# Two matmuls instead of three per k-tile and half in a 32-column projection of a two-layer trunk

## The chip, the core and the metric

The kernel runs on one core of a Trainium2 chip. The time is the device time of one execution in microseconds (us); before the change it is the median of three timed runs. One further execution was recorded by the profiler, and all profile lines of this document come from such recordings.

## The reference, cut to what matters

Two groups of positions, 128 context positions and 512 latent positions, go through two layers. Each layer normalizes, modulates (scale and shift from a condition vector), multiplies by an input weight matrix, runs two mixer branches, gates, and multiplies by an output matrix. In the even layer, one branch is a gated linear attention (GLA) whose gates come from a low-rank projection `rb` of 2 x 16 columns:

```python
qa, ka, va, qb, kb, vb, rb, gp = split_cols(h @ w_in, EVEN_SPLITS)   # rb: 2 * GLA_RANK = 32 columns
...
r = rb.reshape(B, T, 2, GLA_RANK)
logit = jnp.einsum('btdr,drk->btdk', r, wg) + bg
g = (jax.nn.log_sigmoid(logit.astype(jnp.float32)) / GLA_NORMALIZER).reshape(B, T, 2, H_B, DK_B)
```

`h` has 2048 features, `h @ w_in` for `rb` is a product of (640 x 2048) by (2048 x 32). Everything is in float32.

## The kernel before, in words

**Layout.** Activations lie with features on the partitions: 2048 features are 16 k-tiles of 128, and each k-tile holds 642 columns: two columns for the shift vectors of the two groups and 640 positions. The columns are worked on in two halves: half 0 has 322 columns (2 shift columns and 320 positions), half 1 has 320 (`cols`). A projection's output chunk is 128 features x 640 positions and accumulates in two PSUM banks, one per half.

**Precision.** Each float32 operand is split into a `hi` part, rounded to the format in which TensorE (PE) takes one pass, and a `lo` part, the remainder. `acth` and `actl` hold the activations' two parts, `whi` and `wlo` the weights'. A product is taken as hi x hi + lo x hi + hi x lo, so three matmuls per k-tile and half (`mm_k`). Plain float32 matmuls exist too, for small sums and transposes; the profile shows two records for each.

**Weights.** They come from DRAM in units of four k-tiles into `wraw`, a buffer of four slots. ScalarE (ACT) writes `whi` (a copy with rounding), then GpSimd (POOL) writes `wlo` by a subtraction. Both go into a ring of 2560 columns, five blocks of 512; a unit frees its space when its last matmul has been issued (`wpump`, `wget`, `wdone`). The rank projection has only 32 columns; its `hi` and `lo` are each written three times side by side, so that M is 96 and the result stands three times on 96 partitions. `gla_rank` turns this into the factors of the gate matmul in `gla_elem`, whose weights `wgs` are prepared for 96 rows in the same way.

**Order.** One Python program writes each engine's instruction order by hand. It walks through a list `acts` of chunks; while it issues a chunk's matmuls it calls `tick` every two k-tiles, which pumps the weights and advances small tasks (generators in `self.tasks`, such as gates, transposes and attention blocks) and one low-priority task that works out the modulation vectors (`ada_task`). A planner (`Pace`) keeps an estimate of when each engine will be done, by fixed costs, and decides from it which step may be issued next; `until` and `bank` let a task wait for an operand or for a free PSUM bank by this estimate. Modulation sums are made either by VectorE (DVE) in one operation, or by POOL (a product, `prod`) and ACT (the sum of that product), when POOL is free by the estimate (`offload`, `collect`). A change of costs early on therefore changes the order of small work later. PSUM banks are shared out by `pj` (three banks for projections here) and `sm` (three banks for small tasks), two more hold modulation rows.

**Around the change.** The first projections of the even layer are six gate chunks, while modulation weights stream in; then comes the rank projection (`add(d["w_rb"], 96, ...)`, chunk of kind "c", `units`), and then for each of four heads k, q and two value chunks. The rank projection's evacuation `lin` multiplies by the row norm `rstd` on DVE and adds the shift on ACT, into `vt`; then `gla_rank` sets the flag `"r"`, for which the first value chunk's evacuation waits.

Of the kernel before, what the change touches and what calls it, by code (L numbers as in the profile page):

```python
# [13 lines left out]
AF = mybir.ActivationFunctionType  # L14
# [5 lines left out]
KT = D // 128  # L20
# [26 lines left out]
LEAD, FIRST = 1, 6  # L47
# [170 lines left out]
class Core:  # L218
# [14 lines left out]
    ("gmlp_gT", 8),  # L233
    ("gla_m1", 128),
    ("gla_mu", 128),
]


class Trunk:
# [9 lines left out]
    def __init__(self, tc, d, es):  # L249
# [32 lines left out]
        at, c = 0, {}  # L282
# [7 lines left out]
        self.bg_g = c["gla_bgT"].rearrange("p (a b) -> p a b", b=4)  # L290
        self.gn, self.mg, self.m1 = c["gla_gT"], c["gmlp_gT"], c["gla_m1"]
        self.mu = c["gla_mu"].bitcast(U32)
        self.act(self.cT, self.cT, AF.Silu)
        self.ident = self.P([128, 128], "ident")
        make_identity(tc.nc, self.ident)
# [239 lines left out]
    def wstart(self, chunks, acts):  # L535
# [15 lines left out]
                        unit(c, j)  # L551
        last = None
        self.both = {c for kind, x in acts if kind == "h" for c in x[:2]}
        seven = {c for kind, x in acts if kind == "s" for c in x}
        for kind, x in acts:
            if kind == "c" and x >= FIRST:
                for k in (0, 4, 8, 12):
                    unit(x, k)
            elif kind == "k":
                seen = set()  # L560
                for c, k in self.skew(*x[:3]):
                    if (c, k - k % 4) not in seen:
                        seen.add((c, k - k % 4))
                        unit(c, k - k % 4)
            elif kind == "h":
                for r in range(2):
                    for c in x[:2]:
                        for k in (0, 4, 8, 12):
                            unit(c, k, r)
            elif kind == "s":  # L570
                last = self.strassen_jobs(*x, last, unit)
# [75 lines left out]
    def wpump(self, force=False):  # L647
# [18 lines left out]
        if job[0] == "add":  # L666
            o, a, b = job[1]()
# [32 lines left out]
            self.live[key] = (a, a + n * M)  # L700
            self.wpat = a + n * M
        hi, lo = hl
        if m < M:
            raw = raw[:, :, None, :].to_broadcast([128, n, M // m, m])
            hi, lo = (x.rearrange("p a (b c) -> p a b c", c=m) for x in hl)
        nc.scalar.activation(hi, raw, AF.Copy)
        eng = nc.vector if key[0] in self.both and self.nsplit % 2 else nc.gpsimd
        eng.tensor_tensor(lo, raw, hi.bitcast(F32), ALU.subtract)
# [52 lines left out]
    def units(self, c, k0, evac):  # L761

        p = []
        for k in range(k0, KT, 4):
            for half in range(2):
                if k == k0:
                    p.append(self.pj())
                for j in range(k, k + 4):
                    self.mm_k(c, j, [(p[half], half)], k0)
                    if j % 2:  # L770
                        self.tick()
                if k + 4 == KT:
                    evac(*((None, p[1]) if half else (p[0], None)))
                    self.drop(p[half])
            self.wdone((c, k, 0))

    @staticmethod
    def skew(c1, c2, order):
# [1307 lines left out]
    def program(self):  # L2086
# [9 lines left out]
        acts = []  # L2096

        def add(w, M, shift, pre, evac):
            seq.append((w, M, shift, pre, evac))
            acts.append(("c", len(seq) - 1))  # L2100
# [77 lines left out]

            return evac

        add(d["w_rb"], 96, True, None, lazy("vt", rows=96, then=lambda x: self.spawn(self.gla_rank(x))))
        for h in range(4):

            def elem(x, h=h):
# [325 lines left out]
        with tc.manual_schedule():  # L2510
# [13 lines left out]
            for kind, x in acts:  # L2524
                if kind == "c":
                    if x >= FIRST:
                        self.chunk(x)
                elif kind == "s":
                    self.spair(*x)
                elif kind == "k":  # L2530
                    self.kpair(*x)
                elif kind == "h":
                    self.hpair(*x)
                else:
                    x()
# [100 lines left out]
def _consts():  # L2636
# [14 lines left out]
        sel[32 * j, 0] = sel[32 * j + 1, 1] = 1  # L2651
    m1 = np.ones((128, 128), f) + np.eye(128, dtype=f)
    mu = (i[:, None] < i[None, :]).astype(f)
    return {"cos": c4, "sin": s4, "emask": em, "sel": sel, "gla_m1": m1, "gla_mu": mu}


def _na_grid():
# [118 lines left out]
```

## Time and profile before

| | |
|---|---|
| median of three timed runs | 2119.41 us (2116.44 to 2121.92) |
| profiled execution, its own time | 2118.93 us |
| its span in the trace | 2117.1 us |
| busy share PE, DVE, POOL, ACT | 97%, 62%, 61%, 51% |
| rank projection in the trace | 144.36 to 158.48 us |

Times in the trace are counted from the span's start. In a group's row stand the source line, the engine, the operation, the tile written and the tiles read, the shapes, the count, the busy time in us and the mean in ns, then the idle time ahead and what ended it. `PEld` are weight loads, which run beside the matmuls of `PE`; `128*96` is a weight block of 128 rows and 96 columns. Matmul durations overlap, so distances of starts tell what one costs. Where helpers issue everything, all rows have the helper's line (L393 is `mm`, L213 the recording layer), and the tiles' names tell the work apart.

### The profile page before, as it was taken

The numbers are of one execution on the slowest core, as the hardware profiler recorded it, in microseconds if no ns is written. First come the engines' busy times: TensorE is split into PE (matmuls) and PEld (weight loads), VectorE is DVE, ScalarE is ACT, GpSimd is POOL, SyncE is SP. The second block draws the span as 40 slices with busy tenths as digits, with TensorE's granted clock in tenths as the row PEclk, the third lists the DMA queues.
The fourth block names the chain that finished last, engine by engine and source line by source line (L and its number), as shares of the span: only waits on it lengthen the run. The fifth ranks groups of instructions, "written<-read, shape, count | busy, mean of one in ns | idle before, by whom it ended". The sixth has DMA issues, their size and how long they took to land. (4 is left out here: it accounts for less than half of the span.)

```text
span 2117.1 us, 40263 instructions
## 1 busy us (share of the span) xinstructions
PE 2058.0 (97%) x14345; PEld 2003.7 (95%) x14345; DVE 1320.0 (62%) x3063; ACT 1071.2 (51%) x2471; POOL 1285.1 (61%) x1082
## 2 busy tenths in 40 slices
PE   7999999999999999999999999999999999999996
PEld 6899999999999999999999999999999999999995
DVE  4856686666556554988666878777454444465335
ACT  5645565454666665543564444444444544454433
POOL 4756564445545544888565656655555577668873
PEclk9999999999999999999999999999999999999998
DMA  9966343336464544576643455444322344354437
GB/s 363 398 226 189 121 158 107 111 119 197 130 206 150 150 136 145 187 229 219 213 130 105 136 160 159 143 139 149 94 81 90 108 139 130 124 202 132 128 95 248
DMA packets 193401, 341.23 MB, mean 161 GB/s; under 512 B 20944, under 2 KB 70192, under 8 KB 193200
## 3 DMA queue, kind: packets, MB, share of 16 engines
q1 hardware_dynamic: 191728, 337.10, 49.4%
q8 instruction: 112, 1.84, 0.4%
q10 hardware_dynamic: 1472, 1.56, 0.2%
q14 instruction: 89, 0.73, 0.1%
HBM read 304.08 MB, written 31.88 MB: 159 GB/s over the span
## 5 line engine op out<-in xcount | busy, mean ns | idle before, releaser
L393 PE MATMUL bank<-acth,whi 128*128 128x320 f32 (+2 forms) x3320 | 1021.5, 318 | 10.6 <-ACT bc L213 2.8
L393 PE MATMUL bank<-actl,whi 128*128 128x320 f32 (+2 forms) x3320 | 994.7, 310 | 3.7 <-DMA actl<-bl_dram 2.1
L393 PE MATMUL bank<-acth,wlo 128*128 128x320 f32 (+2 forms) x3320 | 994.5, 311 | 3.5 <-POOL wlo L213 3.5
L213 POOL TENSOR_TENSOR wlo<-wraw,whi 128x512 fp32r<-128x512 f32 (+1 forms) x452 | 573.6, 1281 | 412.1 <-ACT whi L213 329.8
L393 PEld LDWEIGHTS bank<-acth,whi 128*128 128x128 f32 (+1 forms) x3320 | 617.6, 189 | 20.9 <-ACT bc L213 3.9
L393 PEld LDWEIGHTS bank<-actl,whi 128*128 128x128 f32 (+1 forms) x3320 | 617.4, 189 | 6.9 <-DMA actl<-bl_dram 3.3
L393 PEld LDWEIGHTS bank<-acth,wlo 128*128 128x128 f32 (+1 forms) x3320 | 617.5, 189 | 5.1 <-POOL wlo L213 5.1
L213 POOL TENSOR_TENSOR wlo<-rs,whi 128x384 fp32r<-128x384 f32 x370 | 408.1, 1123 | 183.2 <-ACT whi L213 143.6
L213 ACT ACTIVATE whi<-wraw 128x512 fp32r<-128x512 f32 (+1 forms) x460 | 262.9, 588 | 93.2 <-PE bank L393 60.7
L393 PE MATMUL bank<-eh,wlo 128*128 128x322 f32 (+1 forms) x666 | 207.2, 311 | 2.7 <-POOL wlo L213 2.7
L393 PE MATMUL bank<-eh,whi 128*128 128x322 f32 (+1 forms) x666 | 209.3, 314 | 0.0
L393 PE MATMUL bank<-el,whi 128*128 128x322 f32 (+1 forms) x666 | 206.9, 311 | 0.0
L213 ACT ACTIVATE whi<-rs 128x384 fp32r<-128x384 f32 x370 | 182.0, 514 | 48.5 <-PE bank L393 41.7
L213 DVE TENSOR_TENSOR wraw<-rs 128x768 f32<-128x768 f32 x74 | 98.8, 1335 | 124.7 <-POOL wlo L213 69.9
L213 DVE CUSTOM_DVE_ANT_0 adas<-adas,bank,partg 128x256 bf16<-128x256 f32 (+1 forms) x290 | 156.2, 539 | 12.6 <-DMA adas<-ada_g 5.3
L213 POOL TENSOR_TENSOR prod<-adas,mixrow 128x512 f32<-128x512 f32 x85 | 111.5, 1321 | 70.4 <-ACT prod L213 48.5
L213 ACT ACTIVATE arena<-arena,bc 128x512 f32<-128x512 f32 (+4 forms) x211 | 106.4, 527 | 79.8 <-DVE arena L213 77.0
L393 PEld LDWEIGHTS bank<-eh,wlo 128*128 128x128 f32 x666 | 125.5, 189 | 3.9 <-POOL wlo L213 3.7
L393 PEld LDWEIGHTS bank<-eh,whi 128*128 128x128 f32 x666 | 125.7, 189 | 0.1
L393 PEld LDWEIGHTS bank<-el,whi 128*128 128x128 f32 x666 | 125.8, 189 | 0.0
L213 DVE CUSTOM_DVE_ANT_0 adas<-adas,bank,part 128x512 bf16<-128x512 f32 x151 | 112.4, 744 | 9.8 <-DMA adas<-ada 6.8
L213 ACT ACTIVATE arena<-Y 128x320 f32<-128x320 f32 (+1 forms) x76 | 38.9, 512 | 152.1 <-DVE Y L213 125.9
(218 smaller groups left out, 2480.1 us busy)
## 6 DMA issues: line engine op xcount, KB each, us to landing
wraw<-w_even SPq DMA_DIRECT2D x176, 256.0 KB, 3.4
adas<-ada_g SPq DMA_DIRECT2D x128, 256.0 KB, 3.7
adas<-ada SPq DMA_DIRECT2D x128, 256.0 KB, 3.8
rs<-w_odd SPq DMA_DIRECT2D x50, 384.0 KB, 3.3
wraw<-w_odd SPq DMA_DIRECT2D x74, 256.0 KB, 3.5
wraw<-w_out SPq DMA_DIRECT2D x64, 256.0 KB, 3.9
rs<-w_odd SPq DMA_DIRECT2D x50, 256.0 KB, 3.8
Y<-ada SPq DMA_DIRECT2D x24, 512.0 KB, 7.3
```

The costliest lines, as they stand in the source:

```text
L213: return f(*args, **kw)
L393: self.nc.tensor.matmul(out, lhsT, rhs, start=start, stop=stop, **kw)
```

## The change

The rank projection's unit in the ring is now one block of 64 columns per k-tile, `hi` in the first 32 and `lo` in the other 32, both within `whi`. For each k-tile and half it is multiplied by `acth` and by `actl`, two matmuls with M = 64; this also takes lo x lo, which the three products leave out. A new method `quad` issues it: half 0 over all 16 k-tiles, then half 1, with all four units of weights held until the end; ACT copies each half's bank into a buffer of the ring `gt`. A spawned task then multiplies each copy, in float32, by the constant `rep` (a 32 x 32 identity matrix tiled 4 x 3; its first 64 rows are used), which adds the `hi` and `lo` rows and repeats the sum three times on 96 partitions; the old evacuation works on that result. `rep` comes with the other small constants in one transfer, which grows from 420 to 516 columns.

```diff
--- before.py
+++ after.py
@@ -233,6 +233,7 @@
     ("gmlp_gT", 8),
     ("gla_m1", 128),
     ("gla_mu", 128),
+    ("rep", 96),
 ]
 
 
@@ -290,6 +291,7 @@
         self.bg_g = c["gla_bgT"].rearrange("p (a b) -> p a b", b=4)
         self.gn, self.mg, self.m1 = c["gla_gT"], c["gmlp_gT"], c["gla_m1"]
         self.mu = c["gla_mu"].bitcast(U32)
+        self.rep = c["rep"]
         self.act(self.cT, self.cT, AF.Silu)
         self.ident = self.P([128, 128], "ident")
         make_identity(tc.nc, self.ident)
@@ -551,9 +553,10 @@
                         unit(c, j)
         last = None
         self.both = {c for kind, x in acts if kind == "h" for c in x[:2]}
+        self.stacked = {x for kind, x in acts if kind == "q"}
         seven = {c for kind, x in acts if kind == "s" for c in x}
         for kind, x in acts:
-            if kind == "c" and x >= FIRST:
+            if kind == "q" or kind == "c" and x >= FIRST:
                 for k in (0, 4, 8, 12):
                     unit(x, k)
             elif kind == "k":
@@ -700,9 +703,9 @@
             self.live[key] = (a, a + n * M)
             self.wpat = a + n * M
         hi, lo = hl
-        if m < M:
-            raw = raw[:, :, None, :].to_broadcast([128, n, M // m, m])
-            hi, lo = (x.rearrange("p a (b c) -> p a b c", c=m) for x in hl)
+        if key[0] in self.stacked:
+            hl = hi
+            hi, lo = hl[:, :, :m], hl[:, :, m:]
         nc.scalar.activation(hi, raw, AF.Copy)
         eng = nc.vector if key[0] in self.both and self.nsplit % 2 else nc.gpsimd
         eng.tensor_tensor(lo, raw, hi.bitcast(F32), ALU.subtract)
@@ -773,6 +776,40 @@
                     evac(*((None, p[1]) if half else (p[0], None)))
                     self.drop(p[half])
             self.wdone((c, k, 0))
+
+    def quad(self, c, parts):
+
+        _, M, shift, _, evac = self.chunks[c]
+        units = [(c, k, 0) for k in range(0, KT, 4)]
+        banks = [self.pj(), self.pj()]
+        for half, p in enumerate(banks):
+            cs = self.cols(half, shift)
+            n = cs.stop - cs.start
+            for u in units:
+                w = self.wget(u)
+                for j in range(4):
+                    for i, x in enumerate((self.ah, self.al)):
+                        k = u[1] + j
+                        self.mm(p[:M, :n], w[:, j, :], x[:, k, cs], start=k == i == 0, stop=k == KT - 1 and i == 1)
+                    if j % 2:
+                        self.tick()
+            self.nc.scalar.activation(parts[half][:M, :n], p[:M, :n], AF.Copy)
+            self.drop(p)
+        for u in units:
+            self.wdone(u)
+
+        def work():
+            for half, x in enumerate(parts):
+                cs = self.cols(half, shift)
+                x = x[:M, : cs.stop - cs.start]
+                yield from self.until(x)
+                yield from self.bank()
+                p = self.sm()
+                self.mm(p[:96, : x.shape[1]], self.rep[:M, :], x)
+                evac(*((None, p) if half else (p, None)))
+                yield
+
+        self.spawn(work(), first=True)
 
     @staticmethod
     def skew(c1, c2, order):
@@ -2178,7 +2215,8 @@
 
             return evac
 
-        add(d["w_rb"], 96, True, None, lazy("vt", rows=96, then=lambda x: self.spawn(self.gla_rank(x))))
+        add(d["w_rb"], 64, True, None, lazy("vt", rows=96, then=lambda x: self.spawn(self.gla_rank(x))))
+        acts.append(("q", acts.pop()[1]))
         for h in range(4):
 
             def elem(x, h=h):
@@ -2527,6 +2565,8 @@
                         self.chunk(x)
                 elif kind == "s":
                     self.spair(*x)
+                elif kind == "q":
+                    self.quad(x, [L["gt"].next() for _ in range(2)])
                 elif kind == "k":
                     self.kpair(*x)
                 elif kind == "h":
@@ -2651,7 +2691,8 @@
         sel[32 * j, 0] = sel[32 * j + 1, 1] = 1
     m1 = np.ones((128, 128), f) + np.eye(128, dtype=f)
     mu = (i[:, None] < i[None, :]).astype(f)
-    return {"cos": c4, "sin": s4, "emask": em, "sel": sel, "gla_m1": m1, "gla_mu": mu}
+    rep = np.tile(np.eye(32, dtype=f), (4, 3))
+    return {"rep": rep, "cos": c4, "sin": s4, "emask": em, "sel": sel, "gla_m1": m1, "gla_mu": mu}
 
 
 def _na_grid():
```

## The prediction

> **What bounds the kernel now.** I read the page's list of engines and its slices first, then stretches of the trace, then the groups of the edited instructions, then the waits.
>
> ```profile
> span 2117.1 us, 40263 instructions
> ...
> PE 2058.0 (97%) x14345; PEld 2003.7 (95%) x14345; DVE 1320.0 (62%) x3063; ACT 1071.2 (51%) x2471; POOL 1285.1 (61%) x1082
> ...
> PEclk9999999999999999999999999999999999999998
> ```
>
> TensorE is busy for 97% of the span at full granted clock; the next engine has 62%. Where the missing 3% lie is seen from stretches (columns: length, then busy time and records of PE, PEld, DVE, ACT and POOL, granted clock, DMA share, GB/s):
>
> ```profile
> 0.00:130.00 130.00, 114.35 (x1299) 101.22 (x1300) 80.83 (x160) 71.58 (x161) 77.06 (x69) 0.99 0.96 360
> 130.00:200.00 70.00, 68.34 (x463) 67.77 (x462) 41.20 (x107) 34.23 (x80) 44.01 (x38) 1.00 0.66 203
> 144.36:158.48 14.12, 14.12 (x98) 14.12 (x97) 5.54 (x15) 6.50 (x15) 9.16 (x9) 1.00 0.76 239
> 200.00:420.00 220.00, 215.53 (x1478) 210.45 (x1477) 155.00 (x271) 122.25 (x255) 118.00 (x82) 1.00 0.39 124
> 420.00:800.00 380.00, 375.76 (x2521) 363.40 (x2520) 221.88 (x594) 232.39 (x582) 190.69 (x146) 1.00 0.49 153
> 800.00:1165.00 365.00, 353.90 (x2358) 348.11 (x2358) 265.15 (x580) 180.10 (x391) 249.73 (x214) 1.00 0.56 178
> 1165.00:2065.00 900.00, 897.53 (x6045) 882.89 (x6044) 527.56 (x1307) 414.55 (x977) 589.72 (x522) 1.00 0.41 130
> ```
>
> Up to 130 us the DMA engines are the limit (share 0.96) and PE is idle for 15.6 us. From 130 to 1165 us it is idle for 1.66 + 4.47 + 4.24 + 11.10 = 21.5 us, from 1165 to 2065 us for 2.5 us. The edited projection lies in the third row, 144.36 to 158.48 us, with no PE idle time at all: in that place a matmul less is time less, unless something that PE needs later is not ready sooner.
>
> **What is removed: 32 matmuls.** The projection's first and last matmul, and the first of the next chunk:
>
> ```profile
> 144.36 0.31 PE L393 MATMUL bank<-acth,whi 128*96 128x322 f32 x1
> ...
> 158.33 0.31 PE L393 MATMUL bank<-acth,wlo 128*96 128x320 f32 x1
> 158.48 0.31 PE L393 MATMUL bank<-acth,whi 128*128 128x322 f32 x1
> ```
>
> Between them stand 16 k-tiles x 2 halves x 3 products = 96 matmuls in 14.12 us, 147 ns each. (Durations of 0.31 us overlap; the distance of starts is the price.) The changed kernel issues 16 x 2 x 2 = 64, with 64 weight columns where there were 96 and the same 322 or 320 moving columns. Does the narrower weight block alter the 147 ns? The 463 records of the stretch 130 to 200 us, nearly all 128 columns wide, took 68.34 us, 148 ns each; so 32 columns less moved the distance by 1 ns at most. The loads themselves:
>
> ```profile
> L393 PEld LDWEIGHTS bank<-acth,whi 128*128 128x128 f32 x3288 | 612.5, 189 | 20.9 <-ACT bc L213 3.9 <-DVE arena L213 3.1 <-issue 3.0
> L393 PEld LDWEIGHTS bank<-acth,whi 128*96 128x96 f32 x32 | 5.2, 162 | 0.0
> L398 PEld LDWEIGHTS bank<-ident,arena 128*64 128x64 f32 x16 | 1.8, 111 | 0.0
> ```
>
> They fell from 189 to 162 ns without a shorter distance, so they lie beside the streaming. I take 147 ns: 64 x 0.147 = 9.41 us, a gain of 4.71 us. The ends for the 64-wide distance: 148 ns, and 147 x 111/162 = 101 ns if loads did set it (6.5 us, a gain of 7.6 us). I take the upper end because 96 against 128 columns is the nearest row. [...]
>
> **What is added on PE: two float32 matmuls** that add the hi and lo rows and copy them three times (64 rows in, 96 out, 322 and 320 columns; at most 64 rows of `rep` are read). No such shape is in the trace; the nearest are the float32 sums over ones, two records to a matmul:
>
> ```profile
> 253.57 1.24 PE L393 MATMUL bank<-arena,ones 128*128 128x320 f32 x4
> 254.41 0.55 PE L393 MATMUL bank<-acth,whi 128*128 128x322 f32 x1
> 254.80 0.31 PE L393 MATMUL bank<-actl,whi 128*128 128x322 f32 x1
> ```
>
> The second ordinary matmul starts at 254.80, so the first took its turn at about 254.65, and two float32 matmuls held PE for 254.65 - 253.57 = 1.08 us. By their records alone they end at 254.41 (0.84 us), by their whole duration 1.24 us: the ends. Net on PE: -4.71 + 1.08 = **-3.6 us** (-3.9 to -3.4 with these ends; -6.5 with the other end of the distance).
>
> **The added wait.** Each half's bank is copied to SBUF by ACT before its float32 matmul. Nearest copy, and the queue that could hold it up:
>
> ```profile
> L213 ACT ACTIVATE sums<-bank 128x322 f32<-128x322 f32 x50 | 21.6, 433 | 17.6 <-PE bank L393 17.6
> ...
> L213 ACT ACTIVATE prod<-prod 128x512 f32<-128x512 f32 x104 | 64.6, 622 | 24.9 <-POOL prod L213 24.5
> ```
>
> In the built order, the first float32 matmul stands 6 matmuls of the next chunk behind the projection, the second another 6 behind it. The second half's copy therefore has 12 x 0.147 + 0.54 = 2.3 us to be made; it takes 0.43 us, but two sums of modulation products stand ahead of it on ACT, and those wait for POOL. Everything on PE stands behind these float32 matmuls.
>
> ```profile
> ACT prod L213 <- POOL prod L213: 24.5, 17, 5.1
> ```
> ```profile
> L393 PE MATMUL bank<-r,wgs x16: 302/308/313, 190.4 to 435.6; 96*128 96x320 f32 x16
> ```
>
> I cost the wait at nothing: ACT is busy for 6.50 of 14.12 us there. If that cover is gone, the price is the longest wait for a product less the cover, 5.1 + 0.43 - 2.3 = 3.2 us, which would leave a gain of 0.3 us. The results themselves are not needed early: the gate matmuls first read them at 190 us.
>
> **Weights, banks and DMA.** The four splits shrink from 384 to 128 columns on ACT and POOL. In the changed order all four stand ahead of the shift columns that the projection's first matmul also needs, so their being shorter gains nothing on the path.
>
> ```profile
> L213 POOL TENSOR_TENSOR wlo<-wraw,whi 128x512 fp32r<-128x512 f32 (+1 forms) x452 | 573.6, 1281 | 412.1 <-ACT whi L213 329.8
> ```
>
> All four blocks are now held to the end of the projection (1024 of 2560 ring columns, which leaves three blocks of the next chunk instead of about four); a block lasts PE 24 x 0.147 = 3.5 us and a split takes POOL 1.28 us, so three are cover enough. The `rep` columns make the first small transfer 128 x 96 x 4 B = 49 KB larger: at the 360 GB/s of the first stretch 0.14 us, at most on the path, at least zero; I take 0.1 us.
>
> **What moves.** The host-side planner writes the order, and from here it comes out differently. Comparing the built orders: 30 matmuls fewer of some 13,400 on PE, and the last 6,172 are the same in both, which is the tail from about 1165 us. Before that, only small tasks (transposes, state and gate matmuls) change place by a few matmuls. The modulation products split anew: POOL does 113 instead of 104, VectorE correspondingly fewer.
>
> ```profile
> L213 DVE CUSTOM_DVE_ANT_0 adas<-adas,bank,part 128x512 bf16<-128x512 f32 x151 | 112.4, 744 | 9.8 <-DMA adas<-ada 6.8
> L213 POOL TENSOR_TENSOR prod<-adas,mixrow 128x512 f32<-128x512 f32 x85 | 111.5, 1321 | 70.4 <-ACT prod L213 48.5 <-DMA adas<-gateT 5.8 <-ACT mixrow L213 5.6
> ```
>
> That is 9 x 1.32 = 11.9 us more on POOL, 9 x 0.62 us on ACT and as many short accumulator reads, 9 x 0.74 us less on VectorE. Both have slack over the stretch, so I cost it at nothing; it is the second rival below that uses it.
>
> **Sum.** -4.7 + 1.1 + 0.1 = -3.5 us. The profiled execution took 2118.93 us (span 2117.1 and 1.8 around it), 0.5 us under the median of 2119.41; on the median's level that makes **2115.9 us**, 0.17% less. Timed runs reached from 2116.44 to 2121.92, so about 0.3%, 6.4 us, is what a measurement can tell from no change.
>
> **Rivals.**
> 1. *The new order also loses stalls* (faster). The 21.5 us of PE idle time before 1165 us are drawn anew. The first of them is near the edit:
>
> ```profile
> 176.14 0.41 PE L393 MATMUL bank<-acth,whi 128*128 128x320 f32 x1 [1.56 <-ACT bc L213]
> ```
> ```profile
> 175.40 0.60 ACT L213 ACTIVATE bank<-adas 128x512 f32<-128x512 f32 x1 [2.20 <-DMA adas<-shift_s]
> ```
>
>    There ACT stood at a copy of modulation rows whose DMA was late, and a projection bank came free late. Losing this and one or two more, 5 us in all, gives 2111 us; 2.9 us are enough to pass the bound. Against it: new stalls are as likely as lost ones. 0.20.
> 2. *POOL becomes late* (slower).
>
> ```profile
> PE bank L393 <- POOL wlo L213: 6.2, 8, 1.4
> ```
>
>    Its place is the split of weights from 160 to 1165 us: a product that the planner put in POOL's queue ahead of a `wlo` delays it by 1.32 us, and once the ring's reserve is used up PE waits. All nine: +11.9 us, 2115.9 + 11.9 = 2127.8 us. It decides (over 2125.8) from 9.9 us, eight of nine. For it: PE already waits 8 times for `wlo`, up to 1.4 us. Against: 6.2 us in all. A row makes it dearer:
>
> ```profile
> L213 DVE TENSOR_TENSOR wgs<-arena,wgs x4: 414/886/1359, 147.9 to 375.3; 32x256 fp32r<-32x256 f32 x4
> ```
>
>    The same subtraction takes 414 to 1359 ns, so a VectorE operation can lose 0.9 us, and more POOL work makes this more frequent. [...] 0.13.
> 3. *The gain is absorbed*: PE comes 3.5 us earlier to evacuations, DMAs or copies that don't, the added wait above among them, and stands there. 2119.4 us. Against: PE's idle time in the GLA stage is only 1.66 + 4.47 us in 290. 0.10.
> 4. *Loads set the distance*: a gain of 7.6 - 1.1 - 0.1 = 6.4 us, 2113.0 us, at the bound. [...]
>
> **Numbers.** My forecast has 0.54, with 2112 to 2121 us as its own range (about 4 us of redrawn stalls each way). Faster by over 0.3%: rivals 1 and 4, 0.23; slower: rival 2, 0.13; within: 0.64. To hold 8 in 10 the range reaches into both: 2108.0 (rival 1 with 8 us of stalls gone) to 2126.5 us (rival 2 past its point).
>
> **What would show it.** In the changed profile: 64 matmuls of 128*64 at 147 ns, 9.4 us from first to last; two float32 matmuls of 64*96, together near 1.1 us, with no idle time ahead of them; PE busy time from 130 us on lower by about 3.6 us, and PE idle time from 130 to 1165 us near 21.5 us; the tail from 1165 us unchanged in length. I am wrong if that idle time differs by more than 3 us, if PE waits on `wlo` for much over 6.2 us, or if the 64-wide distance is far from 147 ns.

## The result, and the profile after

The changed kernel took 2126.76 us (median of 5 runs, 2123.49 to 2129.38) against 2120.38 us of before on the same chip (5 runs, 2116.44 to 2121.92): a ratio of 1.0033, with a 95% interval of 1.0018 to 1.0048. It is slower, by 6.4 us. The forecast was 2115.9 us with a range up to 2126.5 us; the measured time is 10.9 us above the forecast and 0.3 us above the end of the range.

The profiled execution took 2129.38 us. The lines of its page that answer those of before:

```profile
span 2127.6 us, 40229 instructions
...
PE 2058.9 (97%) x14317; PEld 2003.3 (94%) x14317; DVE 1321.0 (62%) x3048; ACT 1077.1 (51%) x2488; POOL 1293.9 (61%) x1091
...
PEclk9999999999999999999999999999999999999998
```

On this page nothing seems to have happened: PE is busy for 0.9 us more with 28 records less. (In rows, `arena`, `small`, `bank`, `prod` and `Y` are buffers, `wlo` the weights' low part, `ident` an identity matrix; the bracket gives the idle time ahead of an instruction and what ended it.) The same stretches as before show more (length, then busy time and records of PE, PEld, DVE, ACT, POOL, granted clock, DMA share, GB/s):

```profile
0.00:130.00 130.00, 110.27 (x1275) 96.11 (x1276) 81.91 (x156) 67.94 (x153) 74.15 (x67) 0.99 0.95 352
130.00:200.00 70.00, 67.40 (x430) 64.56 (x429) 35.22 (x93) 36.41 (x87) 42.78 (x39) 0.95 0.65 202
200.00:420.00 220.00, 213.95 (x1466) 210.81 (x1465) 155.95 (x256) 117.65 (x237) 107.35 (x75) 0.98 0.39 117
420.00:800.00 380.00, 375.01 (x2518) 363.72 (x2518) 228.18 (x602) 239.73 (x603) 212.06 (x160) 1.00 0.52 161
800.00:1165.00 365.00, 351.00 (x2310) 343.93 (x2309) 250.25 (x561) 177.69 (x388) 240.17 (x208) 0.98 0.54 174
1165.00:2065.00 900.00, 897.65 (x6048) 882.92 (x6047) 536.34 (x1324) 417.27 (x984) 594.07 (x523) 1.00 0.42 130
148.83:158.20 9.37, 9.37 (x67) 8.64 (x64) 0.90 (x2) 2.15 (x5) 2.51 (x5) 1.00 0.58 193
```

From 130 to 1165 us PE is idle for 2.60 + 6.05 + 4.99 + 14.00 = 27.6 us (21.5 before). The granted clock, 1.00 in all those stretches of before, is 0.95, 0.98, 1.00 and 0.98. After 1165 us the two profiles agree (897.65 and 897.53 us busy of 900). So the loss lies between the projection and 1165 us, in idle time and in the clock. Five short stretches hold the clock's part:

```profile
161.00:169.60 8.60, 6.73 (x23) 5.76 (x23) 4.79 (x12) 5.96 (x16) 6.87 (x6) 0.60 0.59 167
381.00:392.00 11.00, 6.00 (x30) 5.71 (x29) 9.60 (x13) 4.91 (x13) 4.96 (x4) 0.69 0.32 96
815.00:822.00 7.00, 4.27 (x13) 2.56 (x12) 4.26 (x11) 3.57 (x8) 3.85 (x4) 0.76 0.38 116
851.00:860.00 9.00, 6.72 (x35) 6.49 (x34) 5.53 (x10) 4.24 (x11) 5.03 (x4) 0.81 0.26 71
1086.00:1099.00 13.00, 10.21 (x47) 9.27 (x46) 11.76 (x20) 8.74 (x17) 10.23 (x8) 0.74 0.19 59
```

In each, the granted clock fell to half during a stall of PE or within 1.6 us of its end. A stall is here time in which PE has nothing to run because it waits for another engine. The first stall is the wait that the change added; its rows on PE, ACT's queue ahead of it, and the matmuls:

```profile
159.18 0.78 PE L395 MATMUL bank<-arena,small 64*96 64x322 f32 x2
...
160.59 0.63 ACT L213 ACTIVATE prod<-prod 128x512 f32<-128x512 f32 x1 [1.39 <-POOL prod L213]
161.83 0.63 ACT L213 ACTIVATE prod<-prod 128x512 f32<-128x512 f32 x1 [0.51 <-POOL prod L213]
...
162.46 0.41 ACT L213 ACTIVATE arena<-bank 64x320 f32<-64x320 f32 x1
...
162.92 1.38 PE L395 MATMUL bank<-arena,small 64*96 64x320 f32 x2 [1.87 <-ACT arena L213]
```

The second half's copy (162.46) stood behind two product sums that waited for POOL (1.39 and 0.51 us), as the prediction had described, but the cover of 2.3 us was not enough. The other four stalls of PE:

```profile
386.79 0.47 PE L400 MATMUL bank<-ident,Y 128*128 128x128 f32 x1 [5.00 <-DVE Y L213]
...
818.56 1.22 PE L395 MATMUL bank<-arena 128*128 128x512 f32 x1 [2.73 <-ACT arena L213]
...
854.12 0.41 PE L395 MATMUL bank<-acth,whi 128*128 128x320 f32 x1 [2.28 <-DVE arena L213]
...
1089.56 0.56 PE L395 MATMUL bank<-actl,whi 128*128 128x322 f32 x2 [2.22 <-POOL actl L213]
```

Before had no stall above 1.6 us between 130 and 2065 us, and one stretch of half clock there (at 1081.8 us, 3.4 us long, behind stalls of 1.24 and 1.15 us within 3 us).

Matching the projection matmuls of the two traces one by one, from the first of the edited projection on, gives the position of the changed kernel against before (us; negative is ahead; where small tasks have changed place the position swings by several us for a while, so the places given are ones where it has settled, to about 1 us):

```
end of the projection     -4.8
behind the 2nd float32    +2.0    (the added wait, two float32 matmuls, half clock)
at 178 us of before       +0.2
260 to 380 us             -3.0
387 us                    +2.8    (the 5.00 us stall and half clock)
804 us                    +1.2
816 us                    +6.0    (the 2.73 us stall and half clock)
850 us                    +8.1    (the 2.28 us stall and half clock)
1137 us                   +8.9    (the 2.22 us stall and half clock)
```

At 380 us the changed kernel was still ahead by 3.0 us, about what had been forecast, but by another way: it had been 2.0 us behind and regained 5 us, 1.8 us of it at the stall that before has at 176 us. The loss came behind 380 us, at four stalls.

The projection began 4.5 us later than in the profile of before (148.83 against 144.36 us), and behind 1137 us the changed kernel was 2.9 us shorter: 4.5 + 8.9 - 2.9 = 10.5 us, the difference of the spans. The first and the last term are not the change's doing alone: c_const below, with the instructions of before, has a start 4.3 us later and an end 1.7 us shorter too.

### The profile page after: what moved, and what is told of

Same layout as the page of the kernel before. It is cut to its first block, busy times and chain, and to the rows that moved or that the text cites. A ratio compares the mean times of both kernels' runs of the same rounds, so it can differ in the third digit from the quotient of the medians.

```text
span 2127.6 us, 40229 instructions
## 1 busy us (share of the span) xinstructions
PE 2058.9 (97%) x14317; PEld 2003.3 (94%) x14317; DVE 1321.0 (62%) x3048; ACT 1077.1 (51%) x2488; POOL 1293.9 (61%) x1091
## 3 DMA queue, kind: packets, MB, share of 16 engines
q8 instruction: 112, 1.84, 0.4%
## 5 line engine op out<-in xcount | busy, mean ns | idle before, releaser
L395 PE MATMUL bank<-acth,wlo 128*128 128x320 f32 (+1 forms) x3288 | 986.4, 311 | 3.3 <-POOL wlo L213 3.3
L395 PEld LDWEIGHTS bank<-acth,wlo 128*128 128x128 f32 x3288 | 614.4, 190 | 4.6 <-POOL wlo L213 4.6
L213 POOL TENSOR_TENSOR prod<-adas,mixrow 128x512 f32<-128x512 f32 x93 | 122.5, 1326 | 77.2 <-ACT prod L213 43.6
L213 DVE CUSTOM_DVE_ANT_0 adas<-adas,bank,part 128x512 bf16<-128x512 f32 x143 | 106.4, 744 | 18.9 <-DMA adas<-ada 12.9
L213 DVE TENSOR_TENSOR bank<-bank,sums 128x320 f32<-128x320 f32 (+1 forms) x148 | 70.9, 493 | 70.5 <-PE bank L395 55.2
```

The costliest lines, as they stand in the source:

```text
L213: return f(*args, **kw)
L395: self.nc.tensor.matmul(out, lhsT, rhs, start=start, stop=stop, **kw)
```

## The experiments

To compare profiles, I split each at the first matmul of the projection and at the first matmul of the second layer's chunk that reads `eh` (1137.1 us in before): head, middle, rest.

```
            head    middle   rest     time, us (median)   ratio to before
before     144.4    992.7   980.0     2120.4
after      148.8   1001.6   977.1     2126.8              1.0033 [1.0018, 1.0048]
e1_kept    147.2    991.6   978.8     2121.9              1.0015 [1.0006, 1.0024]
e3_late    145.8   1000.2   978.1     2123.3              1.0022 [1.0013, 1.0032]
p1_minus   145.0    993.8   978.0     2121.9              1.0012 [1.0003, 1.0021]
p3_small   145.0   1000.0   980.3     2129.3              1.0055 [1.0036, 1.0073]
e4_wide    144.6    993.9   978.5     2120.5              0.9995 [0.9987, 1.0004]
c_const    148.7    996.6   978.4     2121.0              1.0003 [0.9992, 1.0013]
e5_vector  146.0    992.4   977.5     2120.1              1.0004 [0.9995, 1.0013]
g_before   146.0    981.6   980.6     2108.4              0.9950 [0.9938, 0.9963]
g_edit     147.2    982.1   980.8     2109.3              0.9953 [0.9940, 0.9967]
```

Head, middle and rest come from one profiled execution each, the time from all timed runs, and the ratio is against before on the same chip in the same session (before's median was 2119.1 to 2120.7 us in these sessions). Up to 1137 us s_long and s_spread (below) run the instructions of before, and so does c_const; with before itself their middles are 992.7, 993.9, 992.9 and 996.6 us. So a difference of less than 4 us between two middles says nothing by itself.

My theory after the result, A: the edit gains its 3.6 us, and the planner's new order loses more, in stalls and in the half clock behind them. Against it B: the edit itself costs (the added wait, the float32 matmuls); and C: the larger transfer of constants delays the first 130 us.

### Order alone: the planner charged differently

In p1_minus and p3_small the kernel is before; only the cost that the planner charges for the projection's matmuls is altered, so that it writes another order.

```diff
 def mm(...):
     cost = n / 2190.0 - 0.0008 if ...
+    if r and out.shape[0] == 96:
+        cost *= 0.745          # p1_minus; 0.93 in p3_small
```

> The kernel of before with its old projection; only the planner is told that the projection's matmuls take 25% less (3.6 us), so that the later order is redrawn as by the change. Theory A: the time moves although no work changed, by 2 to 8 us, with the PE stalls and the half-clock stretches of the new order; which sign is not foreseen. Rival B (the edit itself is the cause): 2120.4 us within 1.5 us.

> As the kernel before, the planner is told that the projection takes 7% less (1.0 us). Theory A: the order is redrawn as much as by a large error, so the time moves by 2 to 8 us, in either direction. Rival B: 2120.4 us within 1.5 us.

p3_small took 2129.3 us, 0.55% more than before, with the same 14345 PE records as before; the new order also moved four modulation sums from VectorE to POOL and ACT (108 product sums on ACT where before has 104). That is more than the 2 to 8 us that theory A had allowed. p1_minus came out 0.12% slower (0.03 to 0.21%): the 2121.9 us lie at the edge of what B allowed and under what A asked, so this run decides nothing, although it was told the 3.6 us of the change. A new order can cost much or almost nothing. In p3_small the middle is 1000.0 us, and two of the stalls of the changed kernel stand in the same places:

```profile
384.34 0.47 PE L400 MATMUL bank<-ident,Y 128*128 128x128 f32 x1 [5.02 <-DVE Y L213]
...
815.67 4.54 PE L395 MATMUL bank<-arena 128*128 128x512 f32 x8 [2.72 <-ACT arena L213]
```

Stretches of that profile around them, and the same places in before behind:

```profile
379.00:391.00 12.00, 6.98 (x35) 6.71 (x34) 9.15 (x15) 6.32 (x15) 3.13 (x2) 0.72 0.35 112
813.00:821.00 8.00, 5.33 (x14) 3.39 (x15) 4.26 (x11) 3.02 (x8) 3.82 (x4) 0.79 0.49 164
```
```profile
377.00:389.00 12.00, 10.97 (x80) 10.46 (x79) 8.80 (x14) 7.80 (x17) 5.31 (x4) 1.00 0.50 153
806.00:816.00 10.00, 10.00 (x59) 8.88 (x58) 5.11 (x14) 5.54 (x13) 5.02 (x4) 1.00 0.57 185
```

So an order that differs only because one cost on the host differs by 7% takes at least about as long as the changed kernel. A loss of this size does not need the edit.

### The edit in the old order

e1_kept has the edited projection, but the planner is charged for the old one, so that everything else keeps before's order. The float32 matmuls are put out 6 and 18 matmuls behind the projection. The two halves alternate unit by unit, as in before, so that both banks are finished near the end; in the change half 0 was finished half a projection earlier.

```diff
+ for a, b in ((hi, h), (hi, l), (lo, h)):
+     self.pe(n / 2190.0 - 0.0008, p[half][:M, :n], a, b)      # charge the old three
+ for i, b in enumerate((h, l)):
+     e.tensor.matmul(p[half][:64, :n], hi[:, 0:64], b, ...)   # issue the new two
...
+ self.hooks.append([self.DELAY[half], f])                     # DELAY = (6, 18)
```

> The changed projection (64-wide blocks, two matmuls per k-tile and half, copies, two float32 matmuls), but the planner is charged for the old one: the order of all other work stays that of before. Theory A (the edit itself gains its 3.6 us; the loss comes from the new order, whose longer PE stalls also bring stretches of half clock): 2116.9 us, granted clock as before (0.994), PE idle time from 130 to 1165 us near 21.5 us. Rival B (the edit itself costs: its added wait, the float32 matmuls): 2124 to 2127 us with a half-clock stretch behind the projection. Rival C (the larger constant transfer slows the first 130 us by some 4 us): the projection starts near 148.8 us instead of 144.4, about 2121 us.

It took 2121.9 us, not 2116.9, and is 0.15% slower than before (0.06 to 0.24%). The gain was there at the end of the projection (-4.75 us against before) and gone behind the float32 matmuls (0.0 us). The profile:

```profile
159.98 0.42 ACT L833 ACTIVATE arena<-bank 64x322 f32<-64x322 f32 x1
160.45 0.78 PE L803 MATMUL bank<-arena,small 64*96 64x322 f32 x2 [2.88 <-ACT arena L833]
```

The first half's copy came 2.9 us too late, again behind product sums. Part of A fell with this: the old order alone does not bring the gain to the end. The number alone is nearest to C (2121 us), which c_const tests. This profile is of the fastest of the 11 executions, with a mean granted clock of 0.995; the other ten had 0.993 or 0.994 and took 2120.4 to 2124.6 us, so that there may be half clock behind the stall in those. No profile shows it.

### The float32 matmuls later, in the new order

```diff
+ self.hooks.append([24, f])     # the float32 matmul and its evacuation, 24 matmuls later; planner not told
```

> The changed kernel with its own order, only the two float32 matmuls and the evacuation behind them are issued 24 matmuls (3.5 us) later. Theory A: the PE stall of 1.9 us ahead of the second float32 matmul goes, and with it the half-clock stretch of 6.8 us behind it (3.4 us of work): 2126.8 - 5.3 = 2121.5 us. Rival (the stretch has nothing to do with that stall): 2126.8 - 1.9 = 2124.9 us and the stretch stays.

2123.3 us, a ratio of 1.0022 where the changed kernel has 1.0033: some 2.3 us less and not the 5.3 of theory A, with intervals that overlap. The profile says more than the time: the stall at 161 us and its half clock are gone, the later ones are not (5.01, 2.72 and 2.19 us; the middle is 1000.2 us). Here the price of the float32 matmuls is seen without a stall:

```profile
159.43 0.31 PE L399 MATMUL bank<-acth,wlo 128*128 128x322 f32 x1
159.67 0.78 PE L832 MATMUL bank<-arena,small 64*96 64x322 f32 x2
160.38 0.41 PE L399 MATMUL bank<-acth,whi 128*128 128x322 f32 x1
160.63 0.31 PE L399 MATMUL bank<-actl,whi 128*128 128x322 f32 x1
```

The ordinary matmul of 159.43 has its turn until 0.147 us later, 159.58, and the one of 160.38 until 160.63, so one float32 matmul takes 160.63 - 0.147 - 159.58 = 0.90 us, two 1.8 us. Position against before: -4.76 at the end of the projection, -2.97 behind both. With the wait gone the edit is worth 3.0 us, and the order still loses 10 us from there.

### Larger constants alone

```diff
+    ("rep", 96),      # in the constants of before; read by nothing
```

> Before with the 96 columns of the replication table added to its constants and read by nothing; every engine's instructions are those of before. Theory C (the larger transfer of constants delays the first stage, as the starts of the projection say: 148.8, 147.2 and 145.8 us in the three kernels that carry the table, 144.4 to 145.0 us in the three that don't): projection start 2 to 4 us later than 144.4 us and a time of 2121 to 2123 us. Theory A (the first stage varies from run to run): 2119 us within 1 us, start of the projection 144 to 146 us.

2121.0 us, a ratio of 1.0003 [0.9992, 1.0013]: C, as some 4 us, falls; the interval has room for 2.8 us at most. The profiled execution of this kernel had its projection start at 148.66 us all the same, and a stall of 3.66 us at 178.9 us, with before's instructions; but it was the second slowest of 12 (2125.5 us), and executions of before in the same session spread from 2115.6 to 2125.1 us. The five profiles of kernels that carry the table in their constants start the projection at 145.8 to 148.8 us, the nine others at 144.4 to 147.2 us. By the median of c_const, then, most of the 4.5 us by which the profile after starts later is scatter, its execution being the slowest of the five; that the larger transfer has no part in it is not shown.

### The float32 matmuls later, in the old order; then the copies on VectorE

```diff
- DELAY = (6, 18)                 # e1_kept
+ DELAY = (30, 45)                 # e4_wide; (12, 24) in e5_vector
+ tc.nc.gpsimd.tensor_copy(...)    # rep from the identity, twice; not from the constants
- e.scalar.activation(parts[half][:64, :n], p[half][:64, :n], AF.Copy)
+ e.vector.tensor_copy(parts[half][:64, :n], p[half][:64, :n])      # e5_vector only
```

> The edited projection in the order of before, as in e1_kept, with two alterations: the two float32 matmuls stand 30 and 45 matmuls behind the projection where e1_kept had 6 and 18, and the 32x96 replication table is built on the chip by two small GpSimd copies of the identity and not carried by the constants. Nothing is left out. Theory A (the edit gains 3.6 us of TensorE time and e1_kept lost it again in one stall of 2.88 us, where the copy of the first half's bank stood on ScalarE behind product sums that wait for GpSimd): that stall is gone, and the time is that of e1_kept less 2.9 us, 2119.0 us, or 2117 if e1_kept's later start of the projection (147.15 against 144.36 us) was the larger constant transfer. Theory B (the edit itself costs): 2121 to 2123 us with no stall near the float32 matmuls.

2120.5 us: the same as before, between the 2119.0 us of A and the 2121 to 2123 us of B. The stall moved from the float32 matmul to the next chunk, which needed the bank that the same late copy had not yet given back:

```profile
157.60 0.42 ACT L835 ACTIVATE arena<-bank 64x322 f32<-64x322 f32 x1
158.06 0.41 PE L401 MATMUL bank<-acth,whi 128*128 128x320 f32 x1 [2.13 <-ACT arena L835]
```

> As e4_wide, with the copies of the two banks made by VectorE, where e4_wide has them on ScalarE behind product sums that wait for GpSimd, and the float32 matmuls 12 and 24 matmuls behind the projection. Nothing is left out. In e4_wide TensorE still stood 2.13 us, at the next matmul that needed the bank which the copy had not yet given back. Theory A (the added copy, by its place in ScalarE's queue, is what eats the edit's gain, first through the float32 matmul, then through the bank): no stall above 0.6 us between 150 and 166 us, and 2120.5 - 2.1 = 2118.4 us, some 2 us below before. Theory B (the edit has no gain to give, wherever the copy runs): 2120.5 us, as before.

2120.1 us, again the same as before, as B said. A's condition, no stall over 0.6 us, was not met: VectorE's copy was late by less (1.14 us, behind modulation products that waited for their transfers), and what was left of the gain met the next wait (first row: PE at the float32 matmul; then ACT and PE at the shift row):

```profile
158.47 0.78 PE L805 MATMUL bank<-arena,rep 64*96 64x322 f32 x2 [1.14 <-DVE arena L835]
...
176.00 0.60 ACT L216 ACTIVATE bank<-adas 128x512 f32<-128x512 f32 x1 [2.38 <-DMA adas<-shift_s]
...
176.74 0.41 PE L401 MATMUL bank<-acth,whi 128*128 128x320 f32 x1 [2.20 <-ACT bc L216]
```

It is the stall that the prediction quoted at 176.14 us of before (1.56 us), now 2.20 us: counted from the projection's start PE came 1.7 us earlier and left 1.1 us earlier, so 0.6 us of the gain went there. Positions against before in e5_vector: -4.75 at the end of the projection, -1.7 behind the float32 matmuls, -1.1 at 176 us, -0.9 at 206 us, -0.8 at 256 us, -0.4 at 1137 us.

### Are the transfers what takes the gain back?

Both kernels of this pair bring a quarter of the modulation rows' columns from the fifth transfer of the stage on, and the instructions read old values in the others. g_edit is e5_vector otherwise, g_before is before.

```diff
+ cut = i >= 4 and jobs[0][0] == "b0" and x.shape[1] == 1
+ self.dma(x, y, (x[:, :, :128], y[:, :, :128]) if cut else None)
```

> Before, in which the transfers of modulation rows (the shift rows and the tiles that are multiplied with them) after the first four of the stage from 145 us on bring 128 of their 512 columns; the other 384 columns are left out, and the instructions that read them read old values. Every instruction and its place are those of before. Base for g_edit. Both theories: the stall of TensorE at 174.6 us, which ended on a shift row's transfer, is shorter than its 1.56 us, and the middle (first matmul of the projection to first matmul of the second layer's chunk on the row pieces, 144.36 to 1137.1 us = 992.7 us in before) is 0 to 2 us shorter.

> e5_vector with the same transfers cut to a quarter (the other columns left out), to be compared with g_before. In e5_vector the edit gained only 0.3 us in the middle (992.4 against 992.7 us), and the matmul behind the second stall started at 176.74 us after a shift row that landed late (176.14 us in before). Theory D (the edit's gain is taken back by modulation rows whose transfers set their own pace, at 157 and at 175 us): without that pace TensorE has no stall over 0.6 us at 157 and at 175 us, and the middle is 2.5 to 3.6 us shorter than that of g_before, and so is the time. Theory E (it is lost elsewhere, along the whole stage): still within 1 us of g_before.

D falls. The transfers matter, for both kernels are 10 to 11 us faster. (For g_before 0 to 2 us had been expected; PE's waits for ACT's `arena` fell from 4.8 to 0.8 us and for `wlo` from 4.9 to 1.4 us between 130 and 1165 us.) In g_edit the stalls at 158 and 175 us are down to 0.49 and 0.55 us, and yet its middle is 982.1 us against 981.6 us without the edit. By the five runs each, the means differ by 1.2 us with an interval of -2.1 to +4.4 us; the 2.5 us or more that D forecast as a gain lie outside, though not by much. PE's idle time in the middle is 15.7 us in g_edit and 12.3 us in g_before, 3.4 us more. Some of it:

```profile
158.98 0.78 PE L805 MATMUL bank<-arena,rep 64*96 64x322 f32 x2 [0.49 <-DVE arena L835]
...
175.58 0.41 PE L401 MATMUL bank<-acth,whi 128*128 128x320 f32 x1 [0.55 <-ACT bc L216]
...
837.07 0.41 PE L401 MATMUL bank<-acth,whi 128*128 128x320 f32 x1 [1.18 <-DVE arena L216]
...
959.78 0.41 PE L401 MATMUL bank<-acth,wlo 128*128 128x320 f32 x1 [0.80 <-POOL wlo L216]
```

Its positions against g_before: -4.75, -2.4 behind the float32 matmuls, -1.6 at 176 us, -1.1 at 207 us, -0.6 at 220 us, then flat to 830 us, +1.3 at 960 us and +0.5 at 1127 us, after g_before had stood at half clock for 6.8 us and g_edit for 3.4 us. So some 1.8 us of the 4.7 are the float32 matmuls, and the rest goes in steps of 0.3 to 1 us at waits for other engines. One of those was there before and grew (0.75 to 1.18 us at 837 us); at 158, 175 and 960 us g_before has no wait over 0.2 us. What each of these small waits hangs on was not taken apart.

### The half clock

After's stretches of half clock are one or two grid steps of 3.413 us long (3.41 or 6.83 us), for the trace's record of the granted clock puts their starts on a grid: from 162.69 us the next ones lie 65.0, 192.0, 203.0 and 272.0 times 3.413 us later, and the changes of the clock lie on such a grid within each of the 14 profiles of this study. Theory G says that a grid stretch in which PE is idle for about half is followed by one at half clock. Two kernels put stalls into before, from 1250 to 1530 us where it has nearly none. The small matmuls write into two columns of a bank in use, so results behind them change; the work does not.

```diff
+ e.tensor.matmul(b, x[:, 0:32], x[:, 0:2], ...)
+ e.scalar.activation(x[:32, 0:2], b, AF.Copy)
+ for _ in range(7):                              # s_long, 6 times; none in s_spread, 24 times
+     e.scalar.activation(x, x, AF.Copy)
+ e.tensor.matmul(b, x[:, 0:32], x[:, 0:2], ...)
```

> Before with six stalls put into TensorE's stream between about 1270 and 1510 us, where before has nearly none: a small matmul, a ScalarE copy of its result, seven more ScalarE operations on a scratch tile, and a small matmul that waits for them, about 2.5 us each. Theory G (the clock is set anew on a grid of 3.413 us, and a grid stretch that is idle for about half, 1.7 us or more, is followed by one at half clock, in which matmuls stand 267 ns apart and not 147): of six stalls of 2.5 us some four fill a grid stretch by half; those are followed by half clock at 1.5 us each, and the time is 2119 + 15 + 6 = 2140 us (2136 to 2146). Rival (a stall costs its own length only): 2119 + 15 = 2134 us, and no stretch of half clock there.

> As s_long, but 24 stalls without the seven further ScalarE operations, one every 75 matmuls (11 us), about 0.7 us each: nearly the same idle time of TensorE, spread out. Theory G: no grid stretch of 3.413 us is idle for half, so no half clock among them, and the time is 2119 + 17 = 2136 us, by the stalls' own lengths alone. Rival (each stall brings a slower clock behind it, whatever its length): half clock behind many of them, and over 2150 us.

The last matmuls of all stalls in s_long with their idle time, a stretch behind the first stall, and the full-clock stretch that follows:

```profile
L408 PE MATMUL bank<-scratch 128*32 128x2 f32 x12 | 1.4, 185 | 20.8 <-ACT scratch L407 20.8
```
```profile
1256.00:1259.40 3.40, 3.40 (x15) 3.40 (x14) 0.00 (x0) 0.23 (x1) 1.68 (x2) 0.50 0.48 142
1259.40:1300.00 40.60, 40.60 (x283) 40.60 (x283) 30.27 (x89) 17.09 (x39) 26.81 (x25) 1.00 0.52 158
```

and of s_spread, with the clock over the whole stretch:

```profile
L408 PE MATMUL bank<-scratch 128*32 128x2 f32 x48 | 5.4, 182 | 13.0 <-ACT scratch L405 13.0
```
```profile
1230.00:1600.00 370.00, 357.02 (x2405) 341.57 (x2405) 240.12 (x740) 160.82 (x415) 201.59 (x184) 1.00 0.41 124
```

All six stalls of s_long (3.0 to 4.3 us, longer than the 2.5 us I had put down) were followed by one grid stretch at half clock: 15 matmul records in 3.4 us, 267 ns from start to start, where 283 took 40.6 us. The excess over 147 ns in these six stretches sums to 8.7 us, 1.45 us each. None of the 24 stalls of s_spread (1.6 us at most) was. Theory G holds. s_long came out at 2156.9 us, above the 2136 to 2146 us expected: its stalls were 20.8 us and not 15, and the small matmuls took some 0.56 us a stall beside them (from one stall's rows). The profile is of its fastest execution, with a mean granted clock of 0.992; the other three had 0.987 to 0.989 and took 2155.8 to 2158.9 us, so those had more half clock; where, no trace shows. s_spread took 2146.0 us: 13.0 us of idle time and about 24 x 0.56 = 13.4 us for the small matmuls, which I had left out.

Over all profiles, between 130 and 2060 us: every grid stretch with 1.86 us or more of PE idle time was followed by half clock, none that ran at full clock with under 1.65 us was, and from 1.65 to 1.84 us it went both ways. e1_kept's stall of 2.88 us fell 1.84 us into one grid stretch and 1.04 us into the next, and had no half clock behind it; after's 1.87 us had 1.65 us in one, and had 6.8 us of it. In seven of the eight cases in which half clock lasted for a second grid stretch PE had been idle for 0.57 us or more in the first; where it ended after one, for 0.52 us or less. The eighth is the one behind 162.69 us, with 0.23 us.

### Why the 5 us stall is so long

VectorE's chain of tensor operations ahead of it in the changed kernel, with POOL's products beside:

```profile
381.34 3.24 POOL L213 TENSOR_TENSOR prod<-adas,mixrow 128x512 f32<-128x512 f32 x2
381.69 1.77 DVE L213 TENSOR_TENSOR arena<-Y 128x640 f32<-128x640 f32 x1
...
383.38 1.88 DVE L213 TENSOR_TENSOR Y<-arena 128x640 f32<-128x640 f32 x1
...
385.19 0.81 DVE L213 TENSOR_TENSOR arena<-Y 128x640 f32<-128x640 f32 x1
```

In the 16 cases of this trace in which POOL ran nothing beside it, the same operation took 0.81 to 0.83 us. f_small shrinks the two products to 64 of their 512 columns and leaves out the rest, in the order of after:

```diff
+ if self.nprod - 1 in (43, 44):
+     self.tc.nc.gpsimd.tensor_tensor(x[:, :64], raw[:, :64], row[:, :64], ALU.mult)
```

> The changed kernel in its own order, in which the two GpSimd products at 381 us take 64 of their 512 columns (the other 448 columns of these two products are left out; the planner is charged for the whole). Theory K (GpSimd's two products and VectorE's two tensor operations beside them hold each other up: 1.77 and 1.88 us in place of 0.82): the two VectorE operations take 0.8 to 0.9 us, and the 5.00 us stall of TensorE before them becomes 3.0 us. Rival (the stall is the order alone, VectorE's scan starting late): the stall stays at 5.0 us. In both a stretch of half clock follows, since over 1.7 us of one grid stretch stay idle.

```profile
376.09 1.36 POOL L1317 TENSOR_TENSOR prod<-adas,mixrow 128x64 f32<-128x64 f32 x2
376.44 0.83 DVE L213 TENSOR_TENSOR arena<-Y 128x640 f32<-128x640 f32 x1
377.19 0.94 DVE L213 TENSOR_TENSOR Y<-arena 128x640 f32<-128x640 f32 x1
...
379.66 0.33 PE L400 MATMUL bank<-ident,Y 128*128 128x128 f32 x1 [3.12 <-DVE Y L213]
```

K holds: 1.9 of the 5.0 us are VectorE and POOL holding each other up, the other 3.1 us are the order, and half clock follows in both (a mean granted clock of 0.92 from 370 to 392 us in f_small). Its time, 2122.99 us, is a single execution and decides nothing. What makes the two engines hold each other up, no run shows.

## Why the prediction was wrong

- **32 matmuls removed, 147 ns each: right.** 64 records of 64 columns took 9.37 us (148.83 to 158.20), 146 ns each. Rival 4 (loads set the distance, 0.03 of the 0.23 for faster) did not come.
- **Two float32 matmuls at 1.08 us: mis-sized.** They take 0.90 us each, 1.8 us together (e3_late). The rows of the sums over ones gave 0.54 us each; the term should have been -4.7 + 1.8 = -2.9 us.
- **"I cost the wait at nothing": wrong.** The mechanism and the queue were named, but only as a worst case of 3.2 us. The reason given, ACT busy for 6.50 of 14.12 us, says nothing of how long a sum at the head of its queue waits; the row quoted beside it has 24.5 us in 17 waits, 1.4 us each, and two such sums stood ahead. It was 1.87 us in the changed kernel, 2.88 us in e1_kept, 2.13 us in e4_wide by way of the bank, 1.14 us in e5_vector with the copy on VectorE. In the changed kernel half clock for 6.8 us came on top, so that the position went from -4.8 to +2.0 us; e3_late, without that wait, was at -3.0 us there.
- **"What moves ... I cost it at nothing": wrong, and this is the step that decided.** I had counted that only small tasks change place by a few matmuls and taken the redrawn stalls as 4 us either way. Four stalls of 2.2 to 5.0 us appeared; PE's idle time rose by 6.2 us, over the 3 us that the prediction named as its own refutation, and the position went from -3.0 us at 380 us to +8.9 us at 1137 us. p3_small shows a loss as large from another order without the edit, with two of the stalls; e3_late, in the order of the change but without the added wait, is still 0.22% slower than before, where the edit in the old order is at best equal. Which stalls a new order brings, nothing in the record lets one foresee: p1_minus, another order, got off with 0.12%.
- **What the prediction lacked altogether** is that a stall costs more than its length. Summing the excess over 147 ns of the distances inside half-clock stretches from the projection to 1165 us gives 13.1 us in after and 1.6 us in before. Some of this is stall that lies inside those stretches; the rest is matmuls at 267 ns.
- **Rival 2 (POOL late on `wlo`) gave 2127.8 us, near the result by luck, for another reason.** PE's waits on `wlo` from 130 to 1165 us came to 5.1 us, against 4.9 before. That a VectorE operation takes longer beside POOL's work, as it said, is seen in before (the `wgs` subtraction took 1.36 us at 217.99 and 375.27 us, beside a split on POOL, and 0.41 us at 147.87 and 294.18 us, with none beside it) and at 381 us of after (1.77 and 1.88 us against 0.81); but it struck VectorE's chain there and not the splits.
- **Rival 3 (the gain is absorbed) is what the edit does in the old order:** e4_wide and e5_vector took as long as before (2120.5 and 2120.1 us), e1_kept 0.15% longer. It had a chance of 0.10, and its argument, little idle time of PE there, did not hold against waits that lengthen when PE comes earlier.
- **Constants at +0.1 us: not contradicted** (c_const, -1.7 to +2.8 us). **The tail from 1165 us unchanged: right in its busy time** (897.65 against 897.53 us); behind 1137 us this profile was 2.9 us shorter, within what other profiles scatter (976.0 to 980.8 us where nothing was put into that part).

No version that computes everything beat before: e4_wide and e5_vector are the same as it within 0.15%. Left open: what the small waits hang on that take back the last 2 to 3 us of the edit in the old order, why before's order has none of the long stalls while p3_small's has, and why p1_minus, with a larger error in the cost, lost so little.

## What to carry to other kernels

Where the order of work comes out of a planner, an edit of a few microseconds redraws the stalls behind it, and here that was worth more than the edit (up to 0.55% from order alone): test the edit with the planner charged for the old work, and the new order with the old work, before believing either. Price a new wait by the queue in which its producer stands and by what the producer's late end holds (here first a matmul, then a bank), and where about 1.7 us or more of a PE stall can fall into one stretch of 3.413 us, count another 1.5 us for the half clock behind it (1.45 us each in s_long). A few matmuls saved ahead of waits that other engines set were taken back here by those waits in steps. And compare several executions: one profile's stages scattered here by 4 us.

## What the runs showed of the hardware that I had not expected

- In the 14 profiles the granted clock changed on a grid of 3.413 us, and about half of one grid stretch idle (always at 1.86 us, never under 1.65 us) was enough for the next to run at half (267 ns a matmul against 147). Whether a stall of 1.9 to 2.9 us cost that hung on where it fell on the grid: e1_kept's 2.88 us did not, after's 1.87 us did.
- A float32 matmul of 64 rows, 96 columns and 320 moving columns held PE for 0.90 us, not the 0.54 us that sums over ones of 128 rows suggested when two stood together; the 0.90 us include the late start of the ordinary matmul behind it (0.41 us long, 0.25 us to the next).
- Two engines' elementwise operations on SBUF stretched each other: VectorE's 0.81 us became 1.77 and 1.88 us beside two POOL products, which took 3.24 us where other pairs in the same trace took 2.5.
- The first 150 us scattered between profiles of kernels with the same instructions there: 144.36, 145.13 and 145.19 us to the same matmul in before, s_spread and s_long, 148.66 us in c_const, whose constants are larger but whose median time is that of before.
